# Opening of a two-layer hybrid decoder kernel: c spread on chip, a dot moved among the squares, eight statistic products, and one more weight tile in the first loop

## The chip, the cores and the metric

The kernel runs on one core of a Trainium2 chip. A core has five engines that run their own instruction streams in order: TensorE (PE in the profile; its weight loads are PEld), VectorE (DVE), ScalarE (ACT), GpSimd (POOL) and SyncE (SP), which here issues most of the DMAs. They wait for one another through semaphores. The metric is the device time of one execution in microseconds (us); lower is better.

## The reference

Two layers on 512 positions of width 1024. `c` is one row of 1024 values that modulates both norms of a layer. Cut to what matters for this change:

```python
c_act = jax.nn.silu(c)
for l in range(DEPTH):                       # DEPTH = 2
    mod = (c_act @ w_ada + b_ada)            # 6 parts of 1024: sh1, sc1, g1, sh2, sc2, g2
    h = rmsnorm(x, norm1_w) * (1 + sc1) + sh1
    u = h @ w_in                             # pool 256, conv 3 x 256, q, k, v 512 each, gates 3 x 1024
    ...                                      # pooling, short convolution, block-sparse attention
    x = x + g1 * (merged @ w_out)
    h2 = rmsnorm(x, norm2_w) * (1 + sc2) + sh2
    x = x + g2 * ((silu(h2 @ w_gate) * (h2 @ w_up)) @ w_down)
```

Here `rmsnorm(x, w)` is `x / sqrt(mean(x*x) + 1e-6) * w`, with the mean over the 1024 features, all in float32.

## The kernel before

Activations are kept transposed: 8 tiles `x[k]` of 128 features by 512 positions. Every matmul of the model is made of three in a reduced float32 form: an operand is split into a rounded part `hi` and a remainder `lo`, and `mm3` (L157) adds hi times hi, hi times lo and lo times hi. Weights come by DMA as `raw` tiles of 7 or 8 blocks of 128 x 128; `split_w` (L323) makes `whi` by a copy on ScalarE (L325) and `wlo = raw - whi` on VectorE (L328). There are 3 `raw` buffers and 5 each of `whi` and `wlo`.

The framework's scheduler orders the instructions of each engine; `pin` keeps an instruction in program order on its engine. In the kernel before, all matmuls, most of VectorE's work and few of ScalarE's instructions are pinned.

**The opening.** DMAs bring `c`, laid out by the host as 128 equal rows (512 KB, tile `csil`, issued by ScalarE), the small parameters `colt` (ScalarE's queue), and the eight `x[k]` (SyncE's queue). ScalarE makes `silu(c)` in place (L207). TensorE does WARM = 22 small products of a ones matrix, which nobody reads. Then the sum of squares: VectorE and ScalarE square the tiles, VectorE adds them in pairs (L675), and TensorE multiplies four sums by the ones matrix into the PSUM tile `scratch[:, 0]`, so that each partition holds the sum over all features. WARM2 = 16 more unread products follow. `ada_first(0, ...)` makes the scale and the shift of feature tile 0: a dot of 128 rows of `w_ada` with `silu(c)` on VectorE (L371), for the part SC1 (the scale) and the part SH1 (the shift), and after each a one-column activation on ScalarE: `am` (L388, the scale with the norm's weight; it reads `abias`) and `mod` (L391, the shift). Then the reciprocal root on ScalarE (L683) and three instructions of a Newton step on VectorE (L684 to L686).

**The normalised tiles.** For tile k: `first_scaled` (VectorE, L490, written `tmp`): x times scale times reciprocal root; `first_hi` (ScalarE, L494): plus shift, rounded; `first_lo` (VectorE, L497): the remainder. Below they are called `scaled`, `hi` and `lo`.

**The first loop of layer 0** runs over k = 0 to 7. In the program, step k emits the two dots of tile k + 2, its `am` and `mod`, its `scaled` and `hi`, the load and the split of the weights of tile k + 2, and its `lo`; then the 21 matmuls of tile k: seven weight blocks (four for q, three feature tiles), each times three, into seven PSUM banks. One of them is `scratch[:, 0]`; the eighth bank, `scratch[:, 1]`, is unused after the warming products. After the loop come feature tiles of 24 matmuls each: `feature_tile` runs over all eight k with one weight tile of eight blocks. The first of them in layer 0 is `pc`, the input of the convolution's first half.

The weights' loads are issued by SyncE in the order of `items`, which `next_w` pops. A tile of the pool `w4` (6 buffers) takes each 512 KB of `w_ada`.

Of the kernel before, what the change touches and what calls it, by code (L numbers as in the profile page):

```python
# [21 lines left out]
P = 128  # L22
D = 1024
S = 512
# [41 lines left out]

WARM = 22

WARM2 = 16

# [5 lines left out]
def hybrid_trunk(ctx, tc, xT, ws, ada, cols, pool_w, qk_w, crow, pos, con, out):  # L78
# [69 lines left out]
    def matmul(*a, **k):  # L148
        tc.keep_in_program_order(T.matmul(*a, **k))  # L149

    def pin(ins):
        return tc.keep_in_program_order(ins)
# [17 lines left out]
    def table(func, after):  # L170

        A.activation(sm([P, 1], tag="tab", bufs=1), after, func)
# [34 lines left out]
    A.activation(csil, csil, AF.Silu)  # L207

# [113 lines left out]

    def split_w(raw, n):  # L323
        hi = wp.tile([P, C_BLOCKS, P], F32R, tag="whi", name=nm("whi"), bufs=5)
        A.activation(hi[:, :n], raw[:, :n], AF.Copy)  # L325
        lo = wp.tile([P, C_BLOCKS, P], F32R, tag="wlo", name=nm("wlo"), bufs=5)
        with tc.issue_after(hold[0].ins) if hold[0] is not None else nullcontext():
            ins = V.tensor_sub(lo[:, :n], raw[:, :n], f32(hi)[:, :n])  # L328
        pin(ins)
        return hi, lo  # L330
# [21 lines left out]
    def wblk(w, b):  # L352
        return w[0][:, b, :], w[1][:, b, :]
# [17 lines left out]
        return V.scalar_tensor_tensor(aw, aw, 1.0, csil, op0=ALU.mult, op1=ALU.mult,  # L371
                                      accum_out=mod[l][:, part, j:j + 1])

    def ada_first_load(j):
        tiles = {}
        for part in (SC1, SH1):
            tiles[part] = w4([P, D])
            nc.sync.dma_start(tiles[part], ada[0, part, j])
        return tiles


# [2 lines left out]
    def ada_first(j, tiles, part):  # L384
        pin(ada_dot(tiles[part], 0, part, j))
        m = mod[0][:, part, j:j + 1]
        if part == SC1:
            A.activation(amod[0][0][:, j:j + 1], m, AF.Identity, scale=colt[:, 0, C_N1 + j:C_N1 + j + 1],  # L388
                         bias=abias[:, j:j + 1])
        else:  # L390
            A.activation(m, m, AF.Identity, bias=colt[:, 0, C_ADA + part * KT + j:C_ADA + part * KT + j + 1])  # L391
# [47 lines left out]
    class Norm:  # L439
# [51 lines left out]
                                       op0=ALU.mult, op1=ALU.mult))  # L491

        def first_hi(self, k):
            A.activation(self.hi[k], self.t, AF.Identity, bias=mod[0][:, SH1, k:k + 1])  # L494

        def first_lo(self, k):
            pin(V.scalar_tensor_tensor(self.lo[k], self.t, mod[0][:, SH1, k:k + 1], f32(self.hi[k]),  # L497
# [168 lines left out]
    pin(V.scalar_tensor_tensor(abias, colt[:, 0, C_ADA + SC1 * KT:C_ADA + (SC1 + 1) * KT], 1.0,  # L666
                               colt[:, 0, C_N1:C_N1 + KT], op0=ALU.add, op1=ALU.mult))
    sq = [bigt(F32) for _ in range(KT)]
    for k in range(KT):
        if k == 0 or (k % 2 == 1 and k < KT - 1):  # L670
            pin(V.tensor_mul(sq[k], x[k], x[k]))
        else:
            A.activation(sq[k], x[k], AF.Square)
# [9 lines left out]
    A.activation(y, scratch[:, 0], AF.Abs_reciprocal_sqrt, bias=epst, scale=1.0 / D)  # L683
    pin(V.scalar_tensor_tensor(t, scratch[:, 0], D * EPS, y, op0=ALU.add, op1=ALU.mult))  # L684
    pin(V.scalar_tensor_tensor(t, t, -0.5 / D, y, op0=ALU.mult, op1=ALU.mult))
    pin(V.scalar_tensor_tensor(norm.rstd, t, 1.5, y, op0=ALU.add, op1=ALU.mult))  # L686
# [16 lines left out]
    for l in range(L):  # L703
# [4 lines left out]
        q_ps = [ps_mm(), pair_a[:, 0], pair_a[:, 1], pair_b[:, 0]]  # L708
        f_ps = [ps_mm(), ps_mm(), ps_mm()]
        held = {}  # L710
        for n, (k, lo, hi) in enumerate([(k, 0, S) for k in range(KT)] if l == 0 else HALVES + REST):
            if l == 0:
                if k + 3 < KT:
                    first.append(ada_first_load(k + 3))
                if k + 2 < KT:
                    ada_first(k + 2, first[k + 2], SC1)
                    ada_first(k + 2, first[k + 2], SH1)
                    norm.first_scaled(k + 2)
                    norm.first_hi(k + 2)
# [102 lines left out]
        for j in range(2):  # L822
            if j == 1:
                pu = ps_mm()
                feature_tile(pu, next_w())
                uc[1] = bigt(F32)
                A.activation(uc[1], pu, AF.Copy)
            pc = ps_mm()
            feature_tile(pc, next_w())
            flush_bulk()  # L830
            z = bigt(F32)
            V.tensor_mul(z, pc, uc[j])
            conv_chain(j, z)
            if j == 1:
                bulk.append((0, lambda: pool_chain(1, pool1)))
# [391 lines left out]
```

## Time and profile before

| | us |
|---|---|
| three runs of the kernel | 1482.32, 1483.5, 1491.17 |
| their median | 1483.5 |
| the profiled execution | 1481.09 |
| its span, first to last instruction | 1479.3 |

The span leaves out what lies around the instructions, 1.8 us. In the rows of the timeline the columns are: start in us from the span's start, duration in us, engine, line of the kernel, operation, the tile written and the tiles read (buffer numbers left out), shapes, how many instructions the row merges, and in brackets the engine's idle time before it and who ended it. Durations of neighbours on one engine can overlap by a few hundredths to tenths of a microsecond, because the engines are pipelined; the distance of two starts is the cost. The chain of waits gives start, length and what was waited for. `L149` is the helper through which all matmuls go, so they are told apart by tiles: `mm`, `pair` are PSUM tiles, `big` are 128 x 512 tiles in SBUF.

### The profile page before, as it was taken

Reading aid. Unit: us, or ns where it says so; the run is one execution under the profiler, and the core shown is the slowest. Engines: PE = TensorE matmul, PEld = TensorE weight load, DVE = VectorE, ACT = ScalarE, POOL = GpSimd, SP = SyncE. Lnnn points to the kernel's source line nnn. Section 1 sums busy time; section 2 is a strip of 40 time slices with the busy share of each in tenths; the row PEclk is TensorE's granted clock in tenths of the full one; section 3 lists DMA queues with packets and bytes.
Section 4 is the critical chain, followed back from the end, with each engine's and each line's share of the span. In section 5 each row is a group of like instructions: output and inputs, shape, how many; then the busy total and the mean of one; then the engine's idle time right before and its main releaser. Section 6 shows DMA issues by size and latency. Waiting matters only on the chain.

```text
span 1479.3 us, 22041 instructions
## 1 busy us (share of the span) xinstructions
PE 1464.6 (99%) x8523; PEld 1276.7 (86%) x8523; DVE 1039.0 (70%) x1791; ACT 659.7 (45%) x1138; POOL 105.7 (7%) x157
## 2 busy tenths in 40 slices
PE   8999999999999999999999999999999999999999
PEld 6888777888988998989988887878889889989997
DVE  7977877766686876767666677877666857657672
ACT  4634444433453352535444345445335534534350
POOL 0000000020000221210000000001100102111200
PEclk9999999999999999999999999999999999999999
DMA  9524444483237775834332243445821436737431
GB/s 352 193 73 164 153 142 144 161 236 104 65 109 219 213 187 170 205 112 117 114 109 89 101 170 130 142 144 181 231 86 54 142 119 165 192 89 197 130 103 68
DMA packets 84409, 217.20 MB, mean 147 GB/s; under 512 B 10832, under 2 KB 23760, under 8 KB 84304
## 3 DMA queue, kind: packets, MB, share of 16 engines
q1 hardware_dynamic: 67456, 177.37, 35.6%
q0 software_dynamic: 16128, 37.76, 11.6%
q8 instruction: 67, 1.10, 0.3%
q10 hardware_dynamic: 720, 0.66, 0.1%
q14 instruction: 38, 0.31, 0.1%
HBM read 213.65 MB, written 2.10 MB: 146 GB/s over the span
## 4 chain that ended last, share of the span: by engine, by line
PE 90%; DVE 5%; ACT 2%; DMA 2%; issue 1%; SPq 0%; DVEq 0%; ACTq 0%
PE mm L149 77%; PE pair L149 11%; PE mm L155 2%; DVE wlo L328 1%; ACT whi L325 1%; DMA raw<-in_ws 1%; DVE raw L371 1%; DMA w<-in_ada 0%; ACT tmp L611 0%; ACT tmp L609 0%; DMA x<-in_xT 0%; DVE w L371 0%; DVE tmp L1060 0%; SPq L232 0%; DVE asm L599 0%
## 5 line engine op out<-in xcount | busy, mean ns | idle before, releaser
L149 PE MATMUL mm<-big,whi 128*128 128x512 f32 (+1 forms) x4362 | 1083.2, 340 | 4.2 <-DVE tmp L1060 2.2
L149 PEld LDWEIGHTS mm<-big,whi 128*128 128x128 f32 x4362 | 745.4, 190 | 92.6 <-DVE tmp L1060 3.8
L149 PE MATMUL mm<-big,wlo 128*128 128x512 f32 (+1 forms) x2181 | 735.9, 337 | 0.0
L149 PEld LDWEIGHTS mm<-big,wlo 128*128 128x128 f32 x2181 | 413.8, 190 | 44.5
L325 ACT ACTIVATE whi<-raw 128x1024 fp32r<-128x1024 f32 (+2 forms) x240 | 248.9, 1039 | 312.8 <-PE mm L149 249.4
L328 DVE TENSOR_TENSOR wlo<-raw,whi 128x1024 fp32r<-128x1024 f32 (+2 forms) x240 | 285.6, 1195 | 111.8 <-ACT whi L325 111.0
L938 DVE SCALAR_TENSOR_TENSOR x<-mm,mod,x 128x512 f32<-128x512 f32 (+1 forms) x90 | 62.1, 691 | 119.1 <-PE mm L149 118.8
L325 ACT ACTIVATE whi<-w 128x1024 fp32r<-128x1024 f32 x72 | 76.2, 1058 | 147.4 <-PE mm L149 100.5
L254 POOL DMA_DIRECT2D w<-in_ws x72 | 46.4, 645 | 1001.4 <-PE mm L149 262.4
L328 DVE TENSOR_TENSOR wlo<-w,whi 128x1024 fp32r<-128x1024 f32 x72 | 86.8, 1221 | 30.7 <-ACT whi L325 30.0
L371 DVE SCALAR_TENSOR_TENSOR raw<-raw,csil 128x1024 f32<-128x1024 f32 x64 | 77.9, 1221 | 4.5 <-DMA raw<-in_ada 4.0
L149 PE MATMUL pair<-whi,big 128*128 128x512 f32 x224 | 76.7, 389 | 0.0
L149 PE MATMUL pair<-big,whi 128*128 128x256 f32 (+1 forms) x376 | 74.0, 294 | 0.0
L256 POOL DMA_DIRECT2D w<-in_ws x72 | 64.3, 925 | 135.3 <-DMA w<-in_ws 125.7
L149 PEld LDWEIGHTS pair<-big,whi 128*128 128x128 f32 x376 | 60.4, 191 | 2.2
L149 PE MATMUL mm<-whi,big 128*128 128x512 f32 x160 | 57.2, 394 | 1.7 <-ACT big L494 1.4
L149 PE MATMUL pair<-big,wlo 128*128 128x256 f32 (+1 forms) x188 | 55.3, 294 | 0.0
L508 DVE TENSOR_TENSOR big<-tmp,big 128x512 fp32r<-128x512 f32 x48 | 33.0, 691 | 24.2 <-ACT big L507 23.2
L149 PEld LDWEIGHTS pair<-whi,big 128*128 128x128 f32 x224 | 42.1, 188 | 8.7
L371 DVE SCALAR_TENSOR_TENSOR w<-w,csil 128x1024 f32<-128x1024 f32 x32 | 38.5, 1223 | 8.4 <-DMA w<-in_ada 8.3
L149 PE MATMUL pair<-wlo,big 128*128 128x512 f32 x112 | 43.7, 390 | 0.0
L625 ACT ACTIVATE w<-mm 128x512 fp32r<-128x512 f32 (+2 forms) x48 | 23.6, 525 | 36.0 <-PE mm L155 35.9
(184 smaller groups left out, 1253.5 us busy)
## 6 DMA issues: line engine op xcount, KB each, us to landing
raw<-in_ws SPq DMA_DIRECT2D x146, 512.0 KB, 3.4
w<-in_ws POOLq DMA_DIRECT2D x144, 256.0 KB, 4.7
raw<-in_ada SPq DMA_DIRECT2D x64, 512.0 KB, 3.3
w<-in_ada SPq DMA_DIRECT2D x32, 512.0 KB, 5.1
raw<-in_ws SPq DMA_DIRECT2D x64, 256.0 KB, 3.9
raw<-in_ws SPq DMA_DIRECT2D x24, 384.0 KB, 3.0
raw<-in_ws SPq DMA_DIRECT2D x16, 448.0 KB, 4.8
raw<-in_ws SPq DMA_DIRECT2D x36, 128.0 KB, 2.8
```

The lines of the kernel that those rows point to most:

```text
L149: tc.keep_in_program_order(T.matmul(*a, **k))
L155: tc.keep_in_program_order(T.transpose(*a))
L254: nc.gpsimd.dma_start(dst, self.source(0, 1))
L256: nc.gpsimd.dma_start(dst, self.source(*other), accum_op=ALU.add)
L325: A.activation(hi[:, :n], raw[:, :n], AF.Copy)
L328: ins = V.tensor_sub(lo[:, :n], raw[:, :n], f32(hi)[:, :n])
L371: return V.scalar_tensor_tensor(aw, aw, 1.0, csil, op0=ALU.mult, op1=ALU.mult, accum_out=mod[l][:, part, j:j + 1])
L508: V.tensor_sub(lo, src, f32(hi))
L625: A.activation(ph[dst], tp, AF.Copy)
L938: V.scalar_tensor_tensor(x[k][:, lo:hi], src, mod[l][:, part, k:k + 1], x[k][:, lo:hi], op0=ALU.mult, op1=ALU.add)
```

## The change

- `c` is loaded as one row of 4 KB into the first partition of `csil`. TensorE spreads it over 128 partitions by two products with a row of ones (in the middle of the warming products, now WARM = 15), and the silu reads the result from PSUM.
- The load of tile 0's SC1 part goes to ScalarE's queue, ahead of `colt`.
- The squares are no longer added in pairs: each of the eight goes into a statistic product of its own. VectorE squares the even tiles, ScalarE the odd ones. `abias` is made after tile 2, and the SC1 dot of tile 0 with its `am` stands after tile 4; the SH1 dot stands behind the reciprocal root in the program.
- More of ScalarE's instructions are pinned: `am`, `mod`, `hi`, the reciprocal root, and `whi` for the first eight loads.
- In layer 0, the weight tile of the first `pc` (`first_part.pop(KT)`) is taken out of the order of loads, fetched in step 1 and split in step 2 of the first loop. From step 2 on its 24 matmuls are done beside the seven blocks, into `scratch[:, 1]`: nine at the end of step 2 (for k = 0, 1, 2), then three at the end of each step. After the loop, `pc` is that bank.

As built, ScalarE's order in each step of the loop is `am`, `mod`, `hi`, `whi`; the eighth tile's `whi` stands right after `whi` of tile 4, its `wlo` right after `lo` of tile 4. Past the first 80 instructions of ScalarE and 115 of VectorE the orders of both kernels are the same.

```diff
-WARM = 22
+WARM = 15
...
-    A.dma_start(csil, crow)
+    A.dma_start(csil[0:1, :], crow[0:1, :])
+    first0 = {SC1: w4([P, D])}
+    A.dma_start(first0[SC1], ada[0, SC1, 0])
     A.dma_start(colt, cols)
...
-    A.activation(csil, csil, AF.Silu)
...
         first_part = [b for b in _plan() if b[0][0] not in ("gate", "up", "down")]
+        if l == 0:
+            extra_blocks = first_part.pop(KT)
...
-        A.activation(hi[:, :n], raw[:, :n], AF.Copy)
+        ins = A.activation(hi[:, :n], raw[:, :n], AF.Copy)
+        if at[0] <= KT:
+            pin(ins)
...
-            A.activation(amod[0][0][:, j:j + 1], m, AF.Identity, scale=colt[:, 0, C_N1 + j:C_N1 + j + 1],
-                         bias=abias[:, j:j + 1])
+            pin(A.activation(amod[0][0][:, j:j + 1], m, AF.Identity, scale=colt[:, 0, C_N1 + j:C_N1 + j + 1],
+                             bias=abias[:, j:j + 1]))
...
         def first_hi(self, k):
-            A.activation(self.hi[k], self.t, AF.Identity, bias=mod[0][:, SH1, k:k + 1])
+            pin(A.activation(self.hi[k], self.t, AF.Identity, bias=mod[0][:, SH1, k:k + 1]))
...
-    for _ in range(WARM):
+    spread = ps_pair()
+    for n in range(WARM):
         matmul(scratch[:, 1, :P], ones, ones, start=True, stop=True)
+        if n == WARM // 2:
+            for h in range(2):
+                matmul(spread[:, h], ones[0:1, :], csil[0:1, h * S:(h + 1) * S], start=True, stop=True)
+    A.activation(csil.rearrange("p (h n) -> p h n", h=2), spread, AF.Silu)
     table(AF.Abs_reciprocal_sqrt, csil[:, 0:1])
-    first = [ada_first_load(0)]
-    pin(V.scalar_tensor_tensor(abias, ...
+    first = [first0]
+    first0.update(ada_first_load(0, (SH1,)))
     sq = [bigt(F32) for _ in range(KT)]
     for k in range(KT):
-        if k == 0 or (k % 2 == 1 and k < KT - 1):
+        if k % 2 == 0:
             pin(V.tensor_mul(sq[k], x[k], x[k]))
         else:
             A.activation(sq[k], x[k], AF.Square)
-        if k % 2 == 1:
-            pin(V.tensor_add(sq[k], sq[k - 1], sq[k]))
-            matmul(scratch[:, 0], ones, sq[k], start=(k == 1), stop=(k == KT - 1))
+        matmul(scratch[:, 0], ones, sq[k], start=(k == 0), stop=(k == KT - 1))
+        if k == 2:
+            pin(V.scalar_tensor_tensor(abias, ...
+        if k == 4:
+            ada_first(0, first0, SC1)
...
-    ada_first(0, first[0], SC1)
+    y, t = bigt(F32), bigt(F32)
+    pin(A.activation(y, scratch[:, 0], AF.Abs_reciprocal_sqrt, bias=epst, scale=1.0 / D))
     ada_first(0, first[0], SH1)
-    y, t = bigt(F32), bigt(F32)
-    A.activation(y, scratch[:, 0], AF.Abs_reciprocal_sqrt, bias=epst, scale=1.0 / D)
...
+        extra, extra_w, done = pair_b[:, 1], None, 0
         for n, (k, lo, hi) in enumerate([(k, 0, S) for k in range(KT)] if l == 0 else HALVES + REST):
...
+            if l == 0 and k == 1:
+                extra_raw = rawt()
+                fetch(extra_raw, l, extra_blocks)
+            if l == 0 and k >= 2:
+
+                if extra_w is None:
+                    extra_w = split_w(extra_raw, KT)
+                while done <= k:
+                    mm3(extra, wblk(extra_w, done), norm.k(done), done == 0, done == KT - 1)
+                    done += 1
...
-            pc = ps_mm()
-            feature_tile(pc, next_w())
+            if l == 0 and j == 0:
+                pc = extra
+            else:
+                pc = ps_mm()
+                feature_tile(pc, next_w())
```

More of the change, by code (lines that the diff above doesn't have):

```diff
@@ L372, in ada_dot, with ada_first_load @@
                                       accum_out=mod[l][:, part, j:j + 1])
-    def ada_first_load(j):
+    def ada_first_load(j, parts=(SC1, SH1), queue=nc.sync):
         tiles = {}
-        for part in (SC1, SH1):
+        for part in parts:
             tiles[part] = w4([P, D])
-            nc.sync.dma_start(tiles[part], ada[0, part, j])
+            queue.dma_start(tiles[part], ada[0, part, j])
         return tiles
@@ L387, in ada_first @@
         if part == SC1:
-            A.activation(amod[0][0][:, j:j + 1], m, AF.Identity, scale=colt[:, 0, C_N1 + j:C_N1 + j + 1],
-                         bias=abias[:, j:j + 1])
+            pin(A.activation(amod[0][0][:, j:j + 1], m, AF.Identity, scale=colt[:, 0, C_N1 + j:C_N1 + j + 1],
+                             bias=abias[:, j:j + 1]))
         else:
-            A.activation(m, m, AF.Identity, bias=colt[:, 0, C_ADA + part * KT + j:C_ADA + part * KT + j + 1])
+            pin(A.activation(m, m, AF.Identity, bias=colt[:, 0, C_ADA + part * KT + j:C_ADA + part * KT + j + 1]))
     def ada_step(l, part, j, early):
@@ L661, in hybrid_trunk @@
     norm = Norm()
-    for _ in range(WARM):
+    spread = ps_pair()
+    for n in range(WARM):
         matmul(scratch[:, 1, :P], ones, ones, start=True, stop=True)
+        if n == WARM // 2:
+            for h in range(2):
+                matmul(spread[:, h], ones[0:1, :], csil[0:1, h * S:(h + 1) * S], start=True, stop=True)
+    A.activation(csil.rearrange("p (h n) -> p h n", h=2), spread, AF.Silu)
     table(AF.Abs_reciprocal_sqrt, csil[:, 0:1])
-    first = [ada_first_load(0)]
-    pin(V.scalar_tensor_tensor(abias, colt[:, 0, C_ADA + SC1 * KT:C_ADA + (SC1 + 1) * KT], 1.0,
-                               colt[:, 0, C_N1:C_N1 + KT], op0=ALU.add, op1=ALU.mult))
+    first = [first0]
+    first0.update(ada_first_load(0, (SH1,)))
     sq = [bigt(F32) for _ in range(KT)]
     for k in range(KT):
-        if k == 0 or (k % 2 == 1 and k < KT - 1):
+        if k % 2 == 0:
             pin(V.tensor_mul(sq[k], x[k], x[k]))
@@ L673, in hybrid_trunk @@
             A.activation(sq[k], x[k], AF.Square)
-        if k % 2 == 1:
-            pin(V.tensor_add(sq[k], sq[k - 1], sq[k]))
-            matmul(scratch[:, 0], ones, sq[k], start=(k == 1), stop=(k == KT - 1))
+        matmul(scratch[:, 0], ones, sq[k], start=(k == 0), stop=(k == KT - 1))
+        if k == 2:
+            pin(V.scalar_tensor_tensor(abias, colt[:, 0, C_ADA + SC1 * KT:C_ADA + (SC1 + 1) * KT], 1.0,
+                                       colt[:, 0, C_N1:C_N1 + KT], op0=ALU.add, op1=ALU.mult))
+        if k == 4:
+            ada_first(0, first0, SC1)
     idle = ps_mm()
```

## The prediction, made blind

> **What bounds the kernel now.** I read the page first, then the chain of waits in order of time.
>
> ```profile
> span 1479.3 us, 22041 instructions
> PE 1464.6 (99%) x8523; PEld 1276.7 (86%) x8523; DVE 1039.0 (70%) x1791; ACT 659.7 (45%) x1138; POOL 105.7 (7%) x157
> ...
> 13.22 1.23 DVE w L371 x2
> ...
> 29.63 0.50 PE mm L149
> ```
>
> TensorE is busy 99% of the span. Up to 29.63 us the chain hops between DMA, VectorE and ScalarE; from 29.63 on it runs along TensorE alone. So the change, which ends before 110 us, can only move the moment at which TensorE has done a given number of matmuls. The trace's pace of TensorE and of one step k of layer 0's first loop:
>
> ```profile
> 34.05 0.39 PE L149 MATMUL mm<-whi,big 128*128 128x512 f32 x1
> ...
> 38.81 0.39 PE L149 MATMUL mm<-whi,big 128*128 128x512 f32 x1
> ...
> 34.11 1.22 DVE L371 SCALAR_TENSOR_TENSOR w<-w,csil 128x1024 f32<-128x1024 f32 x1
> ...
> 36.40 0.75 DVE L490 SCALAR_TENSOR_TENSOR tmp<-x,am,big 128x512 f32<-128x512 f32 x1
> 37.06 1.09 DVE L328 TENSOR_TENSOR wlo<-raw,whi 128x896 fp32r<-128x896 f32 x1
> 38.07 0.75 DVE L497 SCALAR_TENSOR_TENSOR big<-tmp,mod,big 128x512 fp32r<-128x512 f32 x1
> 38.73 1.22 DVE L371 SCALAR_TENSOR_TENSOR w<-w,csil 128x1024 f32<-128x1024 f32 x1
> ...
> 35.66 0.94 ACT L325 ACTIVATE whi<-raw 128x896 fp32r<-128x896 f32 x1
> ...
> 37.24 0.73 ACT L494 ACTIVATE big<-tmp,mod 128x512 fp32r<-128x512 f32 x1 [0.43 <-DVE tmp L490]
> ```
>
> TensorE's 21 matmuls of a step take 38.81 - 34.05 = 4.76 us, 0.2267 each. VectorE's step (two dots, `scaled`, `wlo`, `lo`) takes 38.73 - 34.11 = 4.62 us without a hole. The two run neck and neck: `lo` of a step ends at 38.82, as TensorE starts that step. Written two steps ahead, VectorE's work is hardly ahead at all. And `whi` (35.66) comes before `hi` (37.24) on ScalarE, so `wlo` at 37.06 waits for nothing.
>
> **The opening.**
>
> ```profile
> 1.13 6.79 PE L149 MATMUL pair<-ones 128*128 128x128 f32 x44 [1.13 <-POOL ones L197]
> ...
> 1.51 0.63 PE L149 MATMUL pair<-ones 128*128 128x128 f32 x2
> ...
> 1.72 0.63 PE L149 MATMUL pair<-ones 128*128 128x128 f32 x2
> ...
> 4.28 0.51 PE L149 MATMUL pair<-ones 128*128 128x128 f32 x2
> ...
> 5.24 1.06 ACT L207 ACTIVATE csil<-csil 128x1024 f32<-128x1024 f32 x1 [2.56 <-DMA csil<-in_crow]
> ...
> 9.82 1.31 ACT L673 ACTIVATE big<-x 128x512 f32<-128x512 f32 x2 [0.97 <-DMA x<-in_xT]
> ...
> 12.17 1.02 PE L149 MATMUL pair<-big,ones 128*128 128x512 f32 x2
> 12.60 0.59 PE L149 MATMUL pair<-big,ones 128*128 128x512 f32 x1
> ...
> 13.03 3.73 PE L149 MATMUL mm<-ones 128*128 128x128 f32 x32
> ...
> 13.37 0.67 ACT L683 ACTIVATE big<-pair,epst 128x512 f32<-128x512 f32 x1
> ...
> 14.37 0.69 DVE L684 SCALAR_TENSOR_TENSOR big<-pair,big 128x512 f32<-128x512 f32 x1
> ```
>
> Each fp32 product leaves two records. Small ones first follow at 1.72 - 1.51 = 0.21 us; 1.51 is the third, so 4.28 the 16th, and the other 28 of 44 fit into the rest (to 7.92) only at 0.11 or 0.12, the pace of the later 32 too (3.73 us). A 512-wide record takes 12.60 - 12.17 = 0.43. Now 8 warming products (16 records) stand first, the 16th at 4.28; then the spread's 4 records, 4.49 + 1.72 = 6.21; 7 warming products, 14 x 0.11, to 7.77; eight statistic products, 16 x 0.43 = 6.88, to 14.65, and 0.16 until the last is out (12.60 + 0.59 against 13.03): 14.81 against 13.19. Four products more cost more than the pair sums they replace. Their operands are in time if the last squares are done by 13.8. Before, the last square began at 10.5 (two from 9.82 to 11.13), and now 0.5 MB of c less is ahead of it.
>
> The reciprocal root starts at 14.84, the first Newton step at 15.54 instead of 14.37. Only 1.2 of the 1.6 us count, because at 13.22 to 14.37 VectorE was still in the dots; these now lie beside the products. That is the gain of the moved dot, and it is spent. The silu (1.06 us before, from SBUF) and the table load lie under the products too. I cost `abias`'s move, the moved issues (`cont`, `qkw`, `post` now behind the last square, `ada` on ScalarE's queue) and `colt`, which waits for the single row, at nothing: they have until 13 us. Without that cover, each microsecond that the row lands after 4.49 delays all products by one. No row shows so small a load on idle queues; the 512 KB that it replaces landed at 5.24. From 0 to +0.8, and I take 0, since 4 KB is far from 512.
>
> **The pinned order.** The built order of instructions has ScalarE do, in every step, `am`, `mod`, `hi` and only then `whi`; before, `whi` ran while VectorE was in its dots. VectorE's own order is unchanged (`scaled`, `wlo`, `lo`), and `wlo` subtracts `whi`. So in each step VectorE stands until `hi` and `whi` are through:
>
> ```profile
> 46.48 0.72 ACT L494 ACTIVATE big<-tmp,mod 128x512 fp32r<-128x512 f32 x1 [0.43 <-DVE tmp L490]
> 47.11 1.89 ACT L325 ACTIVATE whi<-raw 128x896 fp32r<-128x896 f32 x2
> ...
> 26.85 0.94 ACT L325 ACTIVATE whi<-raw 128x896 fp32r<-128x896 f32 x1
> 27.82 1.09 DVE L328 TENSOR_TENSOR wlo<-raw,whi 128x896 fp32r<-128x896 f32 x1 [0.54 <-ACT whi L325]
> ```
>
> `whi` follows `hi` by 0.63, `wlo` follows `whi` by 0.97. One step: dots 2.29, `scaled` to `hi` 0.84, 0.63, 0.97, `wlo` 1.01, `lo` 0.66 = 6.40 us instead of 4.62. Behind the waiting `wlo` are queued `lo` and the next step's dots; TensorE waits for all of them.
>
> ```profile
> 16.54 0.75 DVE L490 SCALAR_TENSOR_TENSOR tmp<-x,am,big 128x512 f32<-128x512 f32 x1
> ...
> 17.39 0.72 ACT L494 ACTIVATE big<-tmp,mod 128x512 fp32r<-128x512 f32 x1 [1.83 <-DVE tmp L490]
> ...
> 18.16 0.51 PE L149 MATMUL mm<-whi,big 128*128 128x512 f32 x1 [1.40 <-ACT big L494]
> ...
> 18.87 1.22 DVE L371 SCALAR_TENSOR_TENSOR w<-w,csil 128x1024 f32<-128x1024 f32 x1
> ...
> 19.35 0.39 PE L149 MATMUL pair<-whi,big 128*128 128x512 f32 x1
> ...
> 19.58 0.40 PE L149 MATMUL pair<-wlo,big 128*128 128x512 f32 x1
> ...
> 22.81 0.72 ACT L494 ACTIVATE big<-tmp,mod 128x512 fp32r<-128x512 f32 x1
> ...
> 24.24 1.22 DVE L371 SCALAR_TENSOR_TENSOR w<-w,csil 128x1024 f32<-128x1024 f32 x1
> ```
>
> Tile 0: `scaled` at 17.71 (1.17 late), `hi` 0.85 on, 18.56, `whi` 19.19, first matmul 20.2 (18.16 before), `wlo` 20.16, `lo` 21.17, step 1 at 21.83, 2.96 late. Step 1: from its first dot to `hi` 22.81 - 18.87 = 3.94, then 0.63 + 0.97 + 1.01 + 0.66 = 7.21 in all, so step 2 starts at 29.04 (24.24 before). Steps 2, 3 and 4 end at 29.04 + 3 x 6.40 = 48.24.
>
> **The eighth tile.** Its 24 matmuls are moved, not added: tile, bytes and split all existed, so TensorE's work is the same. But TensorE's order puts its first nine right after step 2, and VectorE's order puts its `wlo` after `lo` of step 4: two steps ahead in program order, and VectorE has no lead.
>
> ```profile
> 53.15 2.35 DVE L328 TENSOR_TENSOR wlo<-raw,whi 128x1024 fp32r<-128x1024 f32 x2
> ```
>
> That `wlo` takes some 1.2 us (half of 2.35), 48.24 to 49.45. TensorE has ended step 2 at about 39.9 (`lo` of step 2 ends at 35.5, then 19 matmuls, 4.3), stands to 47.6 (its `whi` comes 0.95 behind step 4's, at 45.60, and lasts some 1.06, like the silu of that width), does the two that need `whi` alone, and goes on at 49.5. From there nothing is late: step 5's operands are there at 55.9, wanted at 62.0; step 7's at 68.7, wanted at 72.9. Weight buffers come free with TensorE's steps, and the loads have the whole pause. Past the loop the order of the engines is again that of before, but for a few small shifts that VectorE's and ScalarE's lead of 10 us covers.
>
> Sum: 192 matmuls in both kernels. Before, the 45th began at 29.63, so the 192nd ended at 29.63 + 148 x 0.2267 = 63.2. After, the 66th begins at 49.5: 49.5 + 127 x 0.2267 = 78.3. **15.1 us later.** The holes that the extra tile could have filled, 18.16 + 44 x 0.2267 = 28.13 against 29.63, were worth 1.5 us at most.
>
> **The clock after the pause.** TensorE stands 7.7 us where it never stood long. The rows show half pace (0.21 against 0.11) only in the first 3.4 us of work; after the stop from 16.76 to 18.16 the pace was full (19.58 - 19.35). What follows 7.7 us of standing no row shows: 0, or the opening's 3.4 us at half pace, which cost 1.6. I take 1.6, as the pause is nearer in kind to the opening than to 1.4 us; below 0 is out, as no row runs faster. The Trainium skill ("TensorE: Matmul & The Clock Gate", Part 1) says that an idle window of about 3.4 us puts the array back to half its clock, until a like window of work; by it the sum has this term, without it not. The opening's change of pace agrees, and no run here shows the fall back.
>
> 15.1 + 1.6 = 16.7 us on a profiled execution of 1481.1 us (span 1479.3 and 1.8 around it): 1497.8. The three runs of before have a median of 1483.5, 2.4 above that execution; from the median it is **1500**, my forecast.
>
> **Rivals.** (1) The clock stays full: 1483.5 + 15.1 = 1498.6. For it: no row of a fall back. Chance 0.17. (2) `whi` does not hold VectorE up, because ScalarE is idle enough to have it early, and steps stay at 4.62: then only the opening's 1.2 and the wait for the eighth tile's `wlo` count. `lo` of step 4 ends at 40.0, `wlo` at 41.2, 192 matmuls at 41.2 + 28.8 = 70.0: 6.8 late, 1490. Against it: the order on ScalarE is fixed and `hi` needs `scaled`. 0.10. (3) More is lost than counted: half pace lasts two such spells, or the row lands late: 1503 to 1506. 0.10. (4) Faster: the 512 KB less decide.
>
> ```profile
> 6.00:7.00 1.00, 1.00 (x12) 1.00 (x11) 0.74 (x3) 0.98 (x2) 0.00 (x0) 1.00 1.05 402
> ```
>
> At 402 GB/s (last column; the queues are full) they are 1.3 us, the dots are out of the way, and the eighth tile fills the 1.5 us of holes: 1483.5 - 2.8 = 1481. It decides if the products end before 11.9 and the eighth tile's split is done by step 2's end; sixteen records of 0.43 speak against the first, VectorE's order against the second. 0.03. The forecast itself has 0.60.
>
> **Numbers.** 1% of 1483.5, about what a measurement of this kernel can tell from no change, is 14.8 us, so the bound is 1498.3. Forecast (1497 to 1503 by the 2.4 us between execution and median) and rival 1 straddle it: three quarters of 0.60, half of 0.17 and all of rival 3 lie above, 0.63. Faster by over 1% has no mechanism, 0.02; the rest, 0.35, is within. Range 1494 to 1505: forecast, rival 1 and most of rival 3, 0.85; rivals 2 and 4 are left out.
>
> **What would show it.** In the changed profile: products end near 14.8; first matmul of the loop near 20.2; VectorE's steps 6.4 apart, with some 1.8 us before each `wlo`, released by `whi`; TensorE idle from about 40 to 47.6, released by `whi`, then by the eighth tile's `wlo`; 512-wide records 0.43 apart for some 3 us after it; the eighth tile's last matmul near 80. It is wrong if TensorE goes from step 2 to the eighth tile without a stop, or if a step stays under 5 us.

## The result, and the profile after

| | before | after |
|---|---|---|
| median | 1483.38 us (4 runs, 1482.32 to 1491.17) | 1502.91 us (4 runs, 1500.01 to 1505.76) |
| ratio after / before, 95% interval | | 1.0125 (1.0106 to 1.0143) |
| profiled execution | 1481.09 us | 1500.01 us |
| its span | 1479.3 us | 1498.2 us |

The changed kernel is slower by 1.25%. The two profiled executions differ by 18.92 us. First the page of the changed kernel:

```profile
span 1498.2 us, 22029 instructions
...
PE 1474.3 (98%) x8521; PEld 1280.8 (85%) x8521; DVE 1036.0 (69%) x1787; ACT 659.4 (44%) x1138; POOL 105.7 (7%) x157
...
PEclk9899999999999999999999999999999999999999
...
L332 DVE TENSOR_TENSOR wlo<-raw,whi 128x1024 fp32r<-128x1024 f32 (+2 forms) x240 | 285.5, 1194 | 124.0 <-ACT whi L327 122.9
```

TensorE's share fell by one point, its granted clock shows a dent in the second of 40 slices (37 to 75 us), and `wlo` has VectorE standing for 124.0 us over the program (111.0 before). The loss has a place. The 192nd matmul of the model (the last of the first eight tiles, in both kernels) starts here, in the timeline before

```profile
63.07 0.39 PE L149 MATMUL mm<-big,wlo 128*128 128x512 f32 x1
```

and in the timelines of TensorE, ScalarE and VectorE after:

```profile
4.84 2.09 PE L149 MATMUL pair<-csil,ones 1*128 1x512 f32 x4
6.87 1.83 PE L149 MATMUL pair<-ones 128*128 128x128 f32 x14
8.53 7.03 PE L149 MATMUL pair<-big,ones 128*128 128x512 f32 x16
...
21.02 0.50 PE L149 MATMUL mm<-whi,big 128*128 128x512 f32 x1 [1.89 <-ACT whi L327]
...
40.63 0.39 PE L149 MATMUL mm<-big,wlo 128*128 128x512 f32 x1
48.37 1.22 PE L149 MATMUL pair<-big,whi 128*128 128x512 f32 x2 [7.35 <-ACT whi L327]
50.34 0.80 PE L149 MATMUL pair<-big,wlo 128*128 128x512 f32 x1 [0.76 <-DVE wlo L332]
...
81.83 0.39 PE L149 MATMUL pair<-big,wlo 128*128 128x512 f32 x1
...
15.66 0.69 ACT L692 ACTIVATE big<-pair,epst 128x512 f32<-128x512 f32 x1 [4.02 <-PE pair L149]
...
39.41 0.73 ACT L498 ACTIVATE big<-tmp,mod 128x512 fp32r<-128x512 f32 x1 [0.43 <-DVE tmp L494]
40.04 0.94 ACT L327 ACTIVATE whi<-raw 128x896 fp32r<-128x896 f32 x1
...
16.38 0.69 DVE L694 SCALAR_TENSOR_TENSOR big<-pair,big 128x512 f32<-128x512 f32 x1 [3.04 <-ACT big L692]
...
36.28 1.22 DVE L375 SCALAR_TENSOR_TENSOR w<-w,csil 128x1024 f32<-128x1024 f32 x1
...
41.01 1.09 DVE L332 TENSOR_TENSOR wlo<-raw,whi 128x896 fp32r<-128x896 f32 x1 [1.69 <-ACT whi L327]
...
42.68 1.22 DVE L375 SCALAR_TENSOR_TENSOR w<-w,csil 128x1024 f32<-128x1024 f32 x1
...
49.07 1.22 DVE L332 TENSOR_TENSOR wlo<-raw,whi 128x1024 fp32r<-128x1024 f32 x1
```

81.83 - 63.07 = 18.76 us: all of the loss but 0.2 lies before this point. The span behind it is 1498.2 - 81.83 = 1416.4 against 1479.3 - 63.07 = 1416.2. Read from the top: the statistic products start at 8.53 and the root at 15.66. VectorE's steps begin at 36.28 and 42.68, 6.40 apart; in between it stands 1.69 us before `wlo`, since `whi` (40.04) comes behind `hi` (39.41) on ScalarE. TensorE ends step 2 at 40.63 + 0.23 = 40.86, stands 7.35 us for the eighth tile's `whi`, does two matmuls, and goes on at 50.34, when that tile's `wlo` (49.07) is there. Then its pace, by the windows view (window, its length, TensorE's busy time and records, granted clock, DMA share, GB/s):

```profile
22.00:23.00 1.00, 0.85 (x2) 0.59 0.49 196
...
25.00:26.00 1.00, 1.00 (x4) 0.71 0.63 162
...
44.00:46.00 2.00, 0.00 (x0) 1.00 0.76 229
46.00:47.00 1.00, 0.00 (x0) 0.53 0.90 352
...
55.00:56.00 1.00, 1.00 (x3) 0.50 0.00 0
56.00:57.00 1.00, 1.00 (x5) 0.85 0.00 0
```

The clock is halved at about 46.1 (0.53 in that window), in the middle of the stop, and comes back at 56.3 (0.85), some 6 us after work went on. An earlier spell at half clock, from 22.2 to 25.6 (0.59 and 0.71), follows the 1.89 us for which TensorE stands before the loop's first matmul. It moved nothing that counts: in the next two steps TensorE still waits for `wlo`, 0.41 us before 29.36 and 0.62 before 35.75.

### The profile page after: what moved, and what is told of

It is laid out like the page before. It is cut to its first block, busy times and chain, and to the rows that moved or that the text cites. A ratio compares the mean times of both kernels' runs of the same rounds, so it can differ in the third digit from the quotient of the medians.

```text
span 1498.2 us, 22029 instructions
## 1 busy us (share of the span) xinstructions
PE 1474.3 (98%) x8521; PEld 1280.8 (85%) x8521; DVE 1036.0 (69%) x1787; ACT 659.4 (44%) x1138; POOL 105.7 (7%) x157
## 4 chain that ended last, share of the span: by engine, by line
PE 89%; DVE 5%; ACT 3%; DMA 2%; issue 1%; SPq 0%; ACTq 0%; POOL 0%; DVEq 0%; POOLq 0%
PE mm L149 75%; PE pair L149 12%; DMA raw<-in_ws 2%; DVE wlo L332 2%; PE mm L155 2%; ACT whi L327 1%; DVE raw L375 1%; DVE w L375 0%; SPq L232 0%; ACT tmp L615 0%; ACT tmp L613 0%; ACT big L498 0%; DVE tmp L1084 0%; DVE tmp L494 0%; DVE asm L603 0%
## 5 line engine op out<-in xcount | busy, mean ns | idle before, releaser
L332 DVE TENSOR_TENSOR wlo<-raw,whi 128x1024 fp32r<-128x1024 f32 (+2 forms) x240 | 285.5, 1194 | 124.0 <-ACT whi L327 122.9
L149 PE MATMUL pair<-big,whi 128*128 128x256 f32 (+1 forms) x392 | 80.4, 302 | 7.4 <-ACT whi L327 7.4
L149 PEld LDWEIGHTS pair<-big,whi 128*128 128x128 f32 x392 | 64.1, 193 | 10.6 <-ACT whi L327 7.8
L149 PE MATMUL pair<-big,wlo 128*128 128x256 f32 (+1 forms) x196 | 59.3, 303 | 0.8 <-DVE wlo L332 0.8
L149 PEld LDWEIGHTS pair<-big,wlo 128*128 128x128 f32 x196 | 37.9, 193 | 2.6 <-DVE wlo L332 1.5
```

## The experiments

Three measures serve for all of them. *Root* is the start of the reciprocal root on ScalarE, the end of the opening; *192nd* is the start of the 192nd matmul as above. Their difference is the first loop. *Rest* is the span less the start of the 192nd. All are us of one profiled execution.

| kernel | span | root | 192nd | 192nd - root | rest |
|---|---|---|---|---|---|
| before | 1479.3 | 13.37 | 63.07 | 49.70 | 1416.2 |
| after | 1498.2 | 15.66 | 81.83 | 66.17 | 1416.4 |
| e1, `whi` not pinned | 1492.0 | 17.14 | 74.42 | 57.28 | 1417.6 |
| e2, tile from step 5 | 1501.2 | 19.42 | 81.31 | 61.89 | 1419.9 |
| e3, filler in the stop | 1500.3 | 19.23 | 83.98 | 64.75 | 1416.3 |
| e4, no eighth tile | 1494.7 | 16.85 | 79.26 | 62.41 | 1415.4 |
| e5, before, one-row warming | 1483.8 | 16.19 | 65.67 | 49.48 | 1418.1 |
| e6, spread over 128 rows | 1501.0 | 18.51 | 84.20 | 65.69 | 1416.8 |
| e7, opening alone | 1484.8 | 15.91 | 65.39 | 49.48 | 1419.4 |
| e8, not pinned, from step 5 | 1487.9 | 19.54 | 69.06 | 49.52 | 1418.8 |
| e9, e8 with the opening mended | 1488.6 | 15.10 | 64.66 | 49.56 | 1423.9 |
| e10, e9 without the tile | 1487.5 | 17.04 | 66.36 | 49.32 | 1421.1 |
| e11, before, delayed | 1486.0 | 16.05 | 65.50 | 49.45 | 1420.5 |
| e12, before, delayed more | 1501.4 | 32.31 | 83.93 | 51.62 | 1417.5 |

### The pinned copies, the tile, the cold pace

**e1** takes the pin from `whi`.

```diff
-        ins = A.activation(hi[:, :n], raw[:, :n], AF.Copy)
-        if at[0] <= KT:
-            pin(ins)
+        A.activation(hi[:, :n], raw[:, :n], AF.Copy)
```

> The changed kernel without the pin on whi: ScalarE's order puts whi ahead of hi again, the eighth tile stays where it is. Marker: the moment at which TensorE has done 192 matmuls of the model, 63.2 us in the kernel before and 82.1 in the changed one. Theory (opening, pinned whi, the wait for the eighth tile's wlo and the clock's fall each cost on their own): VectorE's steps are back at 4.6 us, TensorE still stops after step 2 until wlo of the eighth tile at about 41.3; marker 70 with a full clock and up to 73 with a half one, a profiled execution of 1488 to 1491. Rival (the stop is only a consequence of the slow steps): with steps of 4.6 TensorE runs through to the eighth tile, marker 65, 1483 to 1485. Rival (the pin is harmless, the stop is all): marker stays above 78, 1497 or more.

Measured: 1493.82 us (one run). The first loop takes 57.28 us instead of 66.17: 8.9 us are the pin's. VectorE's steps are 4.62 apart again (31.69 - 27.07, below). The tile's stop is still there, in the timeline and the windows of e1:

```profile
27.07 0.75 DVE L499 SCALAR_TENSOR_TENSOR big<-tmp,mod,big 128x512 fp32r<-128x512 f32 x1
...
31.69 0.75 DVE L499 SCALAR_TENSOR_TENSOR big<-tmp,mod,big 128x512 fp32r<-128x512 f32 x1
...
39.89 0.73 PE L149 MATMUL pair<-big,whi 128*128 128x512 f32 x2 [2.67 <-ACT whi L327]
42.86 0.80 PE L149 MATMUL pair<-big,wlo 128*128 128x512 f32 x1 [2.24 <-DVE wlo L330]
```

```profile
42.00:43.00 1.00, 0.14 (x1) 0.57 0.99 330
...
48.00:49.00 1.00, 1.00 (x4) 0.51 0.87 319
49.00:50.00 1.00, 1.00 (x6) 1.00 0.39 156
```

A stop of 2.67 and 2.24 us with two matmuls between was enough to halve the clock, from 42.1 to 49.0. Without the pin the tile alone costs 57.28 - 49.70 = 7.6 us. Both rivals fall: the stop stays with short steps, and the 192nd matmul comes well before 78. The whole was missed, 1493.82 against 1488 to 1491: here the root came at 17.14, 1.5 us later than in after, and the rest took 1.2 us more.

**e2** leaves the pin and enters the tile's matmuls from step 5 on.

```diff
-                while done <= k:
+                while k >= 5 and done <= k:
```

> The changed kernel with whi still pinned, the eighth tile's split where it was, but its matmuls only from step 5 on: 18 at the end of step 5, then three a step. Theory: no long stop, TensorE follows VectorE's steps of 6.4 us with a hole of some 1.6 us in each, lo of step 7 ends at 69.5 as in the changed kernel, marker 76, clock full throughout; profiled execution 1494. Rival (the stop is all): marker 65 to 67, 1484. Rival (the tile's place is harmless, since VectorE is the bound anyway): marker 80 to 82, 1498 to 1500.

Measured: 1502.94 us (one run), no faster than after, and the 192nd at 81.31. But the opening took 3.76 us longer in this execution (root 19.42); its loop is 4.3 us shorter than after's, about what the stop and the cold pace cost on top of the pin (e4). So the place of the tile's matmuls isn't harmless, though the 192nd lies where that rival had it. The clock was expected full throughout; it was halved for 3.4 us three times, at 26.5 and 60.7 in the loop and at 1105. Another 3.5 us were lost in the rest. That the whole time did not show the gain led to the questions on the opening and on the rest, below.

**e3** puts 28 products that nobody reads into the stop, to keep TensorE at work.

```diff
                     extra_w = split_w(extra_raw, KT)
+                    for _ in range(28):
+                        matmul(extra[:, :P], ones, ones, start=True, stop=True)
```

> The changed kernel with 28 products of the ones matrix, which nobody reads, between step 2 and the eighth tile's matmuls: they fill 6.2 us of the stop of 7.5 us and move nothing else. Theory (the clock fell in the stop and cost about 2.7 us after it): granted clock 1.00 through the stop, records 0.23 apart from the start, marker 79.4, profiled execution 1497 to 1498, and the runs lie closer together than the 5.8 us of the changed kernel. Rival (the clock falls with VectorE's stalls, not with TensorE's rest): clock and marker as in the changed kernel, 1500 and more.

Measured: median 1506.2 us (4 runs, 1497.3 to 1510.82), ratio 1.015 (1.0094 to 1.0205). The clock stayed up through the filler, which ends at 50.9, and fell after two waits of 1.1 and 1.2 us that were left behind it (windows of e3):

```profile
53.00:54.00 1.00, 0.07 (x1) 0.73 0.93 340
...
56.00:57.00 1.00, 1.00 (x4) 0.56 0.30 112
57.00:58.00 1.00, 1.00 (x6) 1.00 0.06 25
```

One spell from 53.5 to 56.9 in place of one from 46.1 to 56.3 (the earlier one, 26.2 to 29.6 here, is in both). The rival falls: VectorE's steps are the same 6.40, and the clock held as long as TensorE had the filler. The loop is 1.4 us shorter than after's, as a shorter spell gives. The runs were expected closer together and lie further apart: a miss. Only the run of 1502.12 us has a trace. The two slowest, 1510.29 and 1510.82, show a mean granted clock of 0.995 against 0.998 and 0.999 in the other two, so they had more half clock; where, is not known.

**e4** has no eighth tile beside the seven; it is done behind the loop, as before.

```diff
-        if l == 0:
-            extra_blocks = first_part.pop(KT)
...
-                while done <= k:
-                    mm3(extra, wblk(extra_w, done), norm.k(done), done == 0, done == KT - 1)
-                    done += 1
```

> The changed kernel without the eighth tile: opening and pins as changed, pc after the loop as before. Theory: the steps stay at 6.4 us, lo of step 7 ends near 68.4, the loop near 72.7, and pc's 24 matmuls come after it: marker 78.2, clock full in the loop, profiled execution 1496. Rival (the tile's early matmuls carry the loss): marker 65 to 66, 1483 to 1485.

Measured: 1496.5 us (one run). The loop takes 62.41: the pin alone costs 62.41 - 49.70 = 12.7 us, seven steps of 6.40 - 4.62 = 1.78 (12.5). With the pin there, the tile adds 66.17 - 62.41 = 3.8 more, half of its 7.6 alone: both hold up the same TensorE. One spell at half clock, 24.5 to 27.9, stands against the expectation of a full one; behind it TensorE still waits 0.62 us for `wlo` in every step from 36.94 on, so it cost the loop nothing.

**e8** undoes both, **e7** has the changed opening and the other pins (`am`, `mod`, `hi`, the root) alone (the diffs of e1 and e2, and of e1 and e4).

> The changed opening alone: no eighth tile beside the seven, and the ScalarE copies for the weights' first halves where the scheduler puts them. Theory (three costs that add up: opening 2.0 at the Newton steps and 0 to 3.8 more by its clock, pinned order 1.78 a step, the tile's stop and cold pace): steps of 4.62 us, the 192nd product of the model ends 2 to 6 us later than in the kernel before (65.2 to 69), by as much as the root is later than 13.2 within 0.5; the whole 1483 to 1487. Rival (the changed opening itself delays the weights, and so the steps): steps of more than 5 us, the marker beyond 70, the whole above 1489.

> The changed kernel with the ScalarE copies not pinned and the eighth tile's products entered from step 5 on instead of step 2: the two repairs together, the tile still there. Theory (the tile is free once TensorE does not meet its products before the split is done): steps of 4.62, no stop of TensorE over 1 us between 22 us and the marker, the 192nd product at 65 to 69, later than in the kernel before by as much as the root; the whole 1483 to 1487, the same as with no tile at all. Rival (the tile's copies, its subtraction and its 512 KB cost by being early, wherever its products stand): steps of over 5 us around the split, or a stop; marker 70 to 75, the whole 1488 to 1494.

```profile
8.78 7.03 PE L149 MATMUL pair<-big,ones 128*128 128x512 f32 x16
...
65.39 0.39 PE L149 MATMUL mm<-big,wlo 128*128 128x512 f32 x1
```

```profile
11.70 7.75 PE L149 MATMUL pair<-big,ones 128*128 128x512 f32 x16
...
69.06 0.39 PE L149 MATMUL pair<-big,wlo 128*128 128x512 f32 x1
```

(first e7, then e8; the statistic products and the 192nd matmul). Measured: 1486.58 and 1489.71 us (one run each). The loops take 49.48 and 49.52, as before's 49.70: without the pin and with the tile entered late, nothing of the loss is left in the loop, and the tile beside the seven is worth nothing either way. e8's whole lies above what was expected, by its opening, whose products start 3 us later than e7's though the code of both openings is the same.

### The opening's clock

The same 16 warming records stand first in after, e1 to e4, e7 and e8. Two of them, by TensorE's timeline, e1 and then e2:

```profile
8.61 8.44 PE L149 MATMUL pair<-big,ones 128*128 128x512 f32 x16
```

```profile
4.84 3.78 PE L149 MATMUL pair<-csil,ones 1*128 1x512 f32 x4
...
11.70 7.62 PE L149 MATMUL pair<-big,ones 128*128 128x512 f32 x16
```

In e2 (and e3, e8) the spread's four records take 3.78 us, half pace, and so do all warming records behind them. In after and e7 the pace doubles within the spread and stays. In e1 and e4 it doubles before the spread and is halved again behind it: 16 records take 8.44 us in e1 and 7.03 in after. In all of them the spread is four records with a single row to sum over.

**e5** asks whether such products count: the kernel before with one-row warming.

```diff
-        matmul(scratch[:, 1, :P], ones, ones, start=True, stop=True)
+        matmul(scratch[:, 1, :P], ones[0:1, :], ones[0:1, :], start=True, stop=True)
```

> The kernel before, with its 22 warming products made from one row of ones in place of 128 (same shape of result, same number). Theory (a product with one row to sum over does not count as work for the clock): the clock does not come up at 4.55 us; the records of the warming products stay 0.21 us apart to the last, which ends near 5.8, the first of the four statistic products runs at half pace, and the root comes at 14 to 15.5 us instead of 13.2; the whole 1484 to 1486. Rival (rows don't matter, the clock only looks whether products run, and the spread in the opening is its phase): the warming records close up from 0.21 to 0.11 at about 4.5 us as before, root at 13.2, the whole 1481 to 1484.

```profile
1.13 9.75 PE L149 MATMUL pair<-ones 1*128 1x128 f32 x44 [1.13 <-POOL ones L197]
10.81 5.28 PE L149 MATMUL pair<-big,ones 128*128 128x512 f32 x8
```

Measured: 1485.56 us (one run). With 128 rows the 44 records took 6.79 us; with one row they take 9.75, half pace to the last, and the statistic products that follow start at half pace too: their records start at 10.81, 11.83, 12.68 and 13.54, and only from 14.21 on 0.43 apart. So products with one row did not bring the clock up in over 9 us; products with 128 rows did in 3.4 in the kernel before and, at the latest, in 5.5 in e11 (38 of them, no stop between). The root came at 16.19, above what was expected; the rival falls. (Pace has to be read from the distance of starts here: the windows view grants 1.00 throughout the opening.) The Trainium skill ("TensorE: Matmul & The Clock Gate", Part 1) describes the window over which work is counted as about 3.4 us long and running free of the program, so that the moment of change differs from run to run; the openings here, which change pace at different points with the same code, agree.

**e6** spreads over 128 rows, 127 of them zero.

```diff
-    A.dma_start(csil[0:1, :], crow[0:1, :])
+    V.memset(csil, 0.0)
     first0 = {SC1: w4([P, D])}
     A.dma_start(first0[SC1], ada[0, SC1, 0])
+    A.dma_start(csil[0:1, :], crow[0:1, :])
...
-                matmul(spread[:, h], ones[0:1, :], csil[0:1, ...
+                matmul(spread[:, h], ones, csil[:, ...
```

> The changed kernel with the row of c spread by products over all 128 rows (127 of them zero, set by one VectorE instruction ahead of the load) instead of over one row. Theory (the products over one row leave the clock unsettled): the clock rises near 4.5 us and stays, the eight statistic products are 0.86 apart from the first, the root comes at 15 to 15.7 us in the profile, the first 82 us cost about what they did in the changed kernel's profile, and the runs lie closer together, 1499 to 1501.5 with the median at about 1500 instead of 1502.9. Rival (rows don't matter): the same scatter, 1500 to 1506, median at 1502 to 1503; the opening's root anywhere from 15.6 to 19.4.

```profile
1.13 3.78 PE L149 MATMUL pair<-ones 128*128 128x128 f32 x16 [1.13 <-POOL ones L200]
5.73 3.75 PE L149 MATMUL pair<-csil,ones 128*128 128x512 f32 x4 [0.81 <-DMA csil<-in_crow]
9.27 2.27 PE L149 MATMUL pair<-ones 128*128 128x128 f32 x14
11.38 7.03 PE L149 MATMUL pair<-big,ones 128*128 128x512 f32 x16
```

Measured: median 1503.07 us (4 runs, 1501.73 to 1503.91), ratio 1.0122 (1.0093 to 1.0151). As a repair it failed: the row waits for the zeroing, TensorE stands 0.81 us, and the spread runs at half pace. The clock came up at about 10.4, among the 14 records from 9.27 on, and stayed up to the loop. That it was low for 9 us with 128-row products as well seems to be the stop's doing: it lies in one of the windows in which work is counted (last section), 3.6 to 7.0, of whose 3.4 us TensorE worked 2.6. In e5 there is no stop. The runs do lie closer together, 2.2 us against 5.8, but at four runs each that is weak evidence, and the median is after's.

### The mended kernel, and a plain delay

**e9** mends everything that was found: e8's two edits, the row spread over 128 rows with the zeroing shared by two engines, ten warming products all ahead of the spread, and pair sums for the first four squares (six statistic products). **e10** is the same without the tile. The diff shows the sums alone; beside what is named, the silu stands behind the second square and the table load behind the fourth.

```diff
-WARM = 15
+WARM = 10
...
+        if k in (1, 3):
+            pin(V.tensor_add(sq[k], sq[k - 1], sq[k]))
+        if k not in (0, 2):
+            matmul(scratch[:, 0], ones, sq[k], start=(k == 1), stop=(k == KT - 1))
```

> The changed kernel with all its costs mended: copies for the weights' first halves not pinned, the eighth tile entered from step 5, the spread over 128 rows (127 zero, each half set by another engine so that the row is held up less), ten warming products all ahead of it, and the first four squares added in pairs so that six statistic products are left. Theory (opening, pinned order and the tile's place are all there is): the clock is up before 9 us, the root comes at 13.5 to 14.5 us, steps of 4.62, no stop over 1 us in the loop, the 192nd product at 63 to 65 us (63.3 in the kernel before), the ratio to the kernel before 0.999 to 1.001. Rival (something of the change costs beside these, the tile's place in PSUM or the loads' order): marker beyond 67, ratio above 1.003.

> The same without the eighth tile beside the seven. Theory (the tile entered late is free and worth nothing): marker within 0.5 us of the run with the tile after taking out the difference of the roots, ratio to the kernel before 0.999 to 1.001. Rival (the tile fills holes of the loop): without it the marker is 1 to 1.5 us later against its root.

Measured: medians 1491.05 us (12 runs, 1483.58 to 1495.79) and 1491.39 us (12 runs, 1485.49 to 1495.48) beside 1484.05 of the kernel before; ratios 1.0037 (1.0022 to 1.0053) and 1.0044 (1.003 to 1.0059). The first loop is as before, 49.56 and 49.32, with the tile and without: so it fills no holes. The root came at 15.10, not by 14.5, since the second pair sum stood behind `abias` on VectorE, which waited for `colt`. But the ratio was expected at 1.000, and here is a miss: in its profile (1490.41 us) the kernel loses 1.6 us up to the 192nd matmul and 7.7 in the rest. Where, the windows of e9 show:

```profile
890.00:895.00 5.00, 2.98 (x17) 0.86 0.30 105
895.00:900.00 5.00, 5.00 (x21) 0.80 0.30 107
...
1090.00:1095.00 5.00, 2.27 (x9) 1.00 0.32 105
```

A hole of 2 us near 893, then one spell at half clock: (1 - 0.86) x 2 x 5 + (1 - 0.80) x 2 x 5 = 3.4 us. Another hole of 2.7 us stands near 1092. The kernel before stands too between 880 and 900, 1.7 us in one piece that ends at 890.9, but without a spell, and not at all near 1092 (its windows):

```profile
880.00:900.00 20.00, 18.29 (x98) 1.00 0.47 161
...
1090.00:1095.00 5.00, 5.00 (x24) 1.00 0.00 0
```

**e11** and **e12** ask whether the change does that, or any delay: the kernel before with more warming products and nothing else.

```diff
-WARM = 22
+WARM = 38
```

(116 in e12.)

> The kernel before with nothing but a delay: 38 warming products in place of 22, so that the statistic products start at about 11.5 us, the root at 15.1 as in the mended kernel, and the 192nd product of the model ends 1.5 to 2 us later (64.8 to 65.3). Theory A (what the mended kernels lose after the marker is chance or phase, which any delay of the start brings along): median 1488 to 1491, late stops near 890 and 1090 us with the clock falling in some runs. Theory B (something in the change's order brings it): median 1485 to 1486.5, as much later as the marker, span less marker 1416 to 1418.

> The kernel before, delayed as much as the changed kernel is: 116 warming products, statistic products from about 28.8 us, root at 32.4, the 192nd product at 81 to 82 us (0 to 1 us less than the delay, since the weights are split by then). If the changed kernel's loss lies in its first 82 us alone, this kernel takes as long as it: median 1500 to 1504, span less marker 1416 to 1419. If the change also loses or gains something later, the medians differ by that, 2 us or more.

e11 measured: median 1489.32 us (5 runs, 1487.69 to 1491.1), ratio 1.0037 (1.0024 to 1.0049). Its windows:

```profile
890.00:895.00 5.00, 3.23 (x20) 0.92 0.38 107
895.00:900.00 5.00, 5.00 (x20) 0.74 0.34 106
...
1085.00:1105.00 20.00, 18.14 (x79) 1.00 0.31 93
```

The same holes (1.8 and 1.9 us) and the same spell at the same places, in a kernel that is only 2.4 us later at the 192nd matmul: 4.9 us of median for 2.4 us of delay. So they come without anything of the change, and theory A stands. It need not cover all: in the two profiles e9 loses 7.7 us in the rest and e11 4.3, and one profile of each can't tell what the other 3.4 are.

The hole near 890 is in every profile of this document, 827 to 829 us behind the 192nd matmul; in after it is 1.6 us and ends at 909.6. What differs is its length and what follows: the clock fell behind it in e5, e9, e10 and e11, where it took 1.76 us or more, and in no other, where it took 1.71 or less. The runs without a trace point the same way, since slower executions of one kernel show a lower mean clock: in e9 1483.58 us at 1.000 and 1495.79 at 0.996, in the kernel before beside it 1481.38 at 1.000 and 1490.03 at 0.996. So such losses belong to the single execution, and a delay of the start can make them more frequent. What sets the length of the hole, and why the one near 1092 is missing in before, after, e3, e4 and e6, is open.

e12 measured: median 1504.47 us (5 runs, 1503.2 to 1508.92), ratio 1.0152 (1.0137 to 1.0168). Its 192nd starts at 83.93, 2.1 later than after's, and 1504.47 - 2.1 = 1502.4 stands beside after's 1502.91: a kernel that is merely so much later takes as long, within the intervals (the medians of before beside the two differ by 1.1 us). The 192nd was expected 2 to 3 us earlier; ScalarE's rows show why it came late:

```profile
51.77 0.95 ACT L325 ACTIVATE whi<-raw 128x896 fp32r<-128x896 f32 x1 [1.36 <-DMA raw<-in_ws]
52.62 0.71 ACT L494 ACTIVATE big<-tmp,mod 128x512 fp32r<-128x512 f32 x1
```

Here `whi` stands ahead of `hi` and waits for a late load, and `hi` waits behind it: the order that the change avoids has a price as well, when a load comes late.

## Why the prediction was right, and where it was short

- **Slower by over 1%, 1500 us**: 1502.91, ratio 1.0125; inside the range, though one of the four runs, 1505.76, is not. For a profiled execution the sum gave 1497.8, and it was 1500.01. The missing 2.2 us are two terms, below.
- **The opening**, Newton 1.17 us late: it was 16.38 - 14.37 = 2.01. The row was not late, so "I take 0" held: no wait stands before the spread, and in e4 its first product starts at 4.47. What was too small is the sum that ends at 7.77. The record at 1.51 is the second, not the third (1.13 is the first of the 44), so 4.28 is the 15th, and the 16th starts at 4.49. The spread began at 4.84 instead of 4.49, and it took 2.03 us instead of 1.72, since the clock was up only within it: its records start at 4.84, 5.49, 5.92 and 6.35. With 0.1 more in the records behind it, the statistic products started at 8.53 instead of 7.77; from there their 7.03 us were as worked out. That the row's products do not count for the clock was in no term; in this profile it cost little, in e2, e3 and e8 the root came 3.6 to 3.9 us later than here.
- **The pinned order**: 6.40 us a step, released by `whi`, as predicted to the hundredth; e1 and e4 show the cause. Rival 2 (the steps stay at 4.62) fell.
- **The eighth tile**: TensorE was to stand from 39.9 to 47.6 and go on at 49.5; it stood from 40.86 to 48.37 and went on at 50.34, each later by the opening's 0.8 to 1.0. Right in mechanism and size.
- **The clock after the pause**: that it is halved was right (rival 1 fell), the size was not. The term was 1.6 us, one spell of 3.4 us, chosen over 0 with the opening alone to go by. From 50.34, 127 matmuls to 81.83 + 0.23 took 31.72 us instead of 28.79: 2.9. The spell lasted from 46.1 to 56.3, of which TensorE worked 6 us. In e1 it was 6.8 us, in e3 and e9 3.4: multiples of 3.4, which fits the free-running window of the Trainium skill ("TensorE: Matmul & The Clock Gate", Part 1). An estimate from that page's window of about 3.4 us: if work that begins inside one has to fill the next before the pace comes back, the cold time after a stop lies between one window and two; the 6 us agree.
- **Rival 3** named what happened in part, at 1503 to 1506: the spell was longer, but the row was not late; the four runs lie at 1500.0 to 1505.8. **Rival 4** (the 512 KB decide) fell: the products end later, not earlier, and the tile fills no hole (e8 against e7).
- **Nothing past the loop**: right for this pair, 1416.4 against 1416.2, and e12 supports it. That it is no rule show e9 and e11.

The parts don't add: pin alone 12.7 us, tile alone 7.6, both 16.5, since one TensorE waits for both at once.

## What to carry to other kernels

Before pinning an instruction on one engine, ask who on another engine waits for what now stands behind it: two chains that are each written two steps ahead are not ahead of anything when the engines run neck and neck. Work moved to an earlier place in TensorE's order is free only if its operands are there by then; entered three steps later, the same tile cost nothing. Price a stop of TensorE with its cold pace, and compare a kernel with one that is merely delayed by as much, before looking for a second cause.

## What the runs showed of the hardware

- Products with a single row to sum over left TensorE at half pace for over 9 us without a stop (e5). Products over 128 rows of which 127 are zero seem to count: in e6 the pace rose 1.1 us after such a spread of 3.5 us ended, and records of the ones matrix alone never brought it up in under 2.9 us (e4).
- Spells at half clock lasted 3.4, 6.8 and 10.2 us (e3 and e9, e1, after); a hole of 1.8 to 2.0 us in the middle of the program was enough for one (e11, e9).
- Within one execution the granted clock changes only at moments that lie whole multiples of 3.41 us apart: in after at 22.18, 25.59, 46.07 and 56.31. Cut into windows at these moments, the traces show it fall behind windows in which TensorE worked for at most 1.65 of the 3.41 us (after 0.90, e3 1.57, e11 1.65), and stay behind those with 1.71 or more (before 1.71, after 1.77); one window with 1.57, 5 us before the end of after, is the exception. With one-row products it fell behind a window full of work (e1, 4.60 to 8.01). So where a hole lies against these windows matters, and not its length alone.
- A delay of 2.4 us at the start cost 4.9 us of the median (e11), one of 20.9 us cost 20.0 (e12: 83.93 - 63.07 against 1504.47 - 1484.46).
